# Up projection that begins with two products of each of four column pairs, weight sums of those pairs on VectorE, and the norm's sums held in memory

## The chip, the cores and the metric

The kernel runs on one core of one Trainium2 chip. The metric is the device time of one execution in microseconds, the median of several runs. Inside the core five engines work side by side, each through its own list of instructions in order: TensorE (PE in the rows; its weight loads are PEld), VectorE (DVE), ScalarE (ACT), GpSimd (POOL) and SyncE (SP), which only issues DMA transfers here. They wait for each other through semaphores.

## The reference

One step of a one-layer hybrid encoder for 1024 prompt rows and 32 sample rows, which the kernel handles as 1056 columns of the transposed activations:

```python
h = rmsnorm(x, g_mix); proj = h @ w_in            # attention, short convolution, gates
merged = sigmoid(ga) * y_attn + sigmoid(gc) * y_conv
x = x + merged @ w_o
f = square(relu(rmsnorm(x, g_ffn) @ w_up)) @ w_down   # 1024 -> 4096 -> 1024
x = x + f
x = x + sigmoid(rmsnorm(x, g_ple) @ w_ple_gate) * (p @ w_ple)
y = rmsnorm(x, g_final)
```

All is in float32. The kernel multiplies with three products of split operands (high times high, high times low, low times high).

## The kernel before

Activations stand as 128 features by 1056 columns. A large product is tiled by Strassen's scheme in Winograd's form. For the up projection (`w_up`, 1024 by 4096) 256 output features form a set, 16 sets in all. In a set the weights are four quarters A11, A12, A21, A22 (rows of even and odd feature blocks, and the two halves of 128 output features), and the activations are four quarters B11, B21 (left half of the columns, 528) and B12, B22 (right half). Instead of eight quarter products the set takes seven: A11·B11, S1·T1, S2·T2, A12·B21, S3·T3, S4·B22 and A22·T4. S1 to S4 are sums of weight quarters, made once a set (`prepare`, L203 the sums on POOL, L107/L108 the high and low parts of A11 and A12, L164/L166 those of the sums). T1 to T4 are sums of activation quarters, made once for all sets (`sums` L155, `all_t`, `part_t` L159/L160). A quarter product runs over two quarters of 264 columns; each is 12 matmuls (`products`, L216 to L218) into one PSUM tile, evacuated by ACT (L241, L245, L249) or DVE (L252, L257, L262).

T1 to T4 need all eight rows of the output projection before it (`output_projection`, whose tiles are `ps_wo`, and whose result is stored, squared into `ssq1` and made into B operands by `operands`, L1329/L1330). So the first set does not use the seven products: `up_plain` runs it as eight plain quarter products (tile `ps_up`) while `all_t` makes T1 to T4, and while POOL and ACT prepare set 1. Sets 1 to 15 follow in order, each by `seven`. The results are squared, and further sums of them (`mid_sums`, L1477 to L1485) go to device memory, from where the down projection (`ps_dn`) fetches them.

The order of the work is written by hand: an instruction stands on its engine where the program issues it. `run` takes one step of the main generator (one quarter product with its evacuation), and after each step one step of every generator in the list `side`: preparing the next set's weights, fetching the weights of the set after that, `all_t`, and `mean_squares` (L1450 to L1455), which turns `ssq1` into the norm's factor `rs2` for the down projection. Weight buffers (`raw`, four of 512 KB) and the high and low parts (`whi`, `wlo`, two each) rotate, so a fetch waits until the low part of the older weights is made.

Between the input projection and the attention two tiles of gates are written to device memory (`gd`, L1129), then come the loads of keys, values and queries (`keys_values`, `queries`, L777 to L779).

## Time and profile before

| what | value |
|---|---|
| median of 3 runs | 1541.56 us (1541.32 to 1542.14) |
| profiled execution, its own time | 1541.38 us |
| its span | 1539.7 us |
| PE busy, PEld busy | 1518.7 us, 1506.5 us |
| DVE, ACT, POOL busy | 1067.1, 750.5, 317.6 us |
| up projection, from first ps_up to first ps_dn | 766.36 to 1098.70 us |

The span is the profiler's, from the first to the last instruction; the execution's own time holds 1.7 us more around it. PE is busy nearly throughout, so the table by engine says little: what counts is how far apart matmuls start, and where PE waits.

### The profile page before, as it was taken

How to read it: one execution, taken by the hardware profiler on the slowest of the kernel's cores; microseconds unless marked ns; L12 is line 12 of the kernel's file. 1: busy time of each engine (PE TensorE's matmuls, PEld its weight loads, DVE VectorE, ACT ScalarE, POOL GpSimd, SP SyncE). 2: the span in 40 equal slices, each digit the busy share in tenths (PEclk: the TensorE clock that was granted, in tenths of full speed). 3: DMA queues.
4: the chain of work that ended last, by engine and by line, in shares of the span. 5: the costliest groups of instructions: out<-in, count | busy, mean ns of one | idle time of the engine just before them, and what ended most of it. 6: DMA issues, size and time to landing. Idle time of an engine off the chain costs nothing.

```text
span 1539.7 us, 29459 instructions
## 1 busy us (share of the span) xinstructions
PE 1518.7 (99%) x11816; PEld 1506.5 (98%) x11816; DVE 1067.1 (69%) x1441; ACT 750.5 (49%) x1371; POOL 317.6 (21%) x340
## 2 busy tenths in 40 slices
PE   8999999999999999999999999999999999999997
PEld 7999999999999999999999999999999999999997
DVE  7568656657578887775577555545577986789756
ACT  6544444434456664432355555555543334434644
POOL 2223322231112221002312222221020220000253
PEclk9999999999999999999999999999999999999999
DMA  6513445413748633445354444344886897683433
GB/s 226 202 48 118 187 153 193 166 44 130 236 125 257 207 123 124 147 167 182 128 191 140 146 147 152 131 143 155 303 281 205 279 332 241 198 275 120 141 127 117
DMA packets 110568, 268.94 MB, mean 175 GB/s; under 512 B 12992, under 2 KB 30144, under 8 KB 110432
## 3 DMA queue, kind: packets, MB, share of 16 engines
q1 hardware_dynamic: 110144, 266.75, 51.3%
q8 instruction: 92, 1.51, 0.4%
q14 instruction: 44, 0.36, 0.1%
q10 hardware_dynamic: 288, 0.32, 0.1%
HBM read 186.31 MB, written 80.72 MB: 173 GB/s over the span
## 4 chain that ended last, share of the span: by engine, by line
PE 63%; DVE 0%; ACT 0%; issue 0%; DVEq 0%
PE ps_dn L1696 7%; PE ps_dn L1698 7%; PE ps_dn L1697 7%; PE ps_A11u L217 4%; PE ps_A11u L216 4%; PE ps_A11u L218 4%; PE ps_pg L116 2%; PE ps_wo L1387 2%; PE ps_wo L1386 2%; PE ps_wo L1385 2%; PE ps_pg L118 2%; PE ps_pg L117 2%; PE ps_S1u L217 2%; PE ps_S1u L218 2%; PE ps_S1u L216 2%; PE ps_oa L116 1%
## 5 line engine op out<-in xcount | busy, mean ns | idle before, releaser
L1698 PE MATMUL ps_dn<-fh,wlo_dn 128*128 128x264 f32 x896 | 255.0, 285 | 0.0
L1696 PE MATMUL ps_dn<-fh,whi_dn 128*128 128x264 f32 x896 | 254.8, 284 | 0.0
L1697 PE MATMUL ps_dn<-fl,whi_dn 128*128 128x264 f32 x896 | 254.5, 284 | 0.0
L1696 PEld LDWEIGHTS ps_dn<-fh,whi_dn 128*128 128x128 f32 x896 | 168.8, 188 | 0.0
L1698 PEld LDWEIGHTS ps_dn<-fh,wlo_dn 128*128 128x128 f32 x896 | 168.6, 188 | 0.0
L1697 PEld LDWEIGHTS ps_dn<-fl,whi_dn 128*128 128x128 f32 x896 | 168.6, 188 | 0.0
L203 POOL TENSOR_TENSOR s_i<-raw_i,raw_i 128x512 f32<-128x512 f32 x32 | 43.6, 1363 | 239.9 <-DVE slS_i L166 209.8
L809 DVE TENSOR_TENSOR_SCAN r<-r 128x128 f32<-128x128 f32 (+3 forms) x64 | 86.4, 1351 | 4.1 <-POOL r L802 4.1
L1583 ACT CAST whi_dn<-raw_dn 128x1024 fp32r<-128x1024 f32 x40 | 42.0, 1051 | 83.5 <-PE ps_dn L1697 83.5
L203 POOL TENSOR_TENSOR s_u<-raw_u,raw_u 128x512 f32<-128x512 f32 x30 | 44.1, 1470 | 182.7 <-DVE slS_u L166 171.0
L1589 DVE TENSOR_TENSOR wlo_dn<-raw_dn,whi_dn 128x1024 fp32r<-128x1024 f32 x40 | 61.3, 1532 | 28.4 <-ACT whi_dn L1583 28.4
L216 PE MATMUL ps_A11i<-T,shS_i 128*128 128x264 f32 x256 | 73.1, 285 | 0.0
L218 PE MATMUL ps_A11i<-T,slS_i 128*128 128x264 f32 x256 | 72.9, 285 | 0.0
L217 PE MATMUL ps_A11i<-T,shS_i 128*128 128x264 f32 x256 | 72.7, 284 | 0.0
L849 DVE TENSOR_TENSOR at<-pa,at 128x512 fp32r<-128x512 f32 (+2 forms) x96 | 52.0, 551 | 26.7 <-ACT at L848 22.2
L1609 DVE TENSOR_TENSOR fl<-mr,fh 128x1056 fp32r<-128x1056 f32 x56 | 70.0, 1249 | 0.3 <-ACT q L1649 0.3
L166 DVE TENSOR_TENSOR slS_i<-s_i,shS_i 128x512 fp32r<-128x512 f32 x48 | 35.1, 737 | 49.7 <-ACT shS_i L164 49.5
L802 POOL TENSOR_SCALAR_AFFINE_SELECT r<-r 128x128 f32<-128x128 f32 x64 | 30.4, 475 | 187.8 <-ACT r L795 176.4
L1780 POOL TENSOR_TENSOR xx<-xx,pgs 128x384 f32<-128x384 f32 (+1 forms) x23 | 24.2, 1057 | 216.8 <-DVE pgs L1779 210.1
L216 PE MATMUL ps_A11u<-T,shS_u 128*128 128x264 f32 x240 | 68.4, 285 | 0.0
L217 PE MATMUL ps_A11u<-T,shS_u 128*128 128x264 f32 x240 | 68.4, 285 | 0.0
L218 PE MATMUL ps_A11u<-T,slS_u 128*128 128x264 f32 x240 | 68.1, 284 | 0.0
(451 smaller groups left out, 5582.9 us busy)
## 6 DMA issues: line engine op xcount, KB each, us to landing
raw_dn<-in_w_down_dram SPq DMA_DIRECT2D x56, 512.0 KB, 4.5
raw_i<-in_w_in_dram SPq DMA_DIRECT2D x36, 512.0 KB, 4.6
mr<-mdT SPq DMA_DIRECT2D x32, 528.0 KB, 5.5
raw_u<-in_w_up_dram SPq DMA_DIRECT2D x32, 512.0 KB, 3.5
mdB<-m SPq DMA_DIRECT2D x48, 264.0 KB, 2.5
mr<-mdB SPq DMA_DIRECT2D x24, 528.0 KB, 6.2
raw_pg<-in_w_ple_gate_dram SPq DMA_DIRECT2D x17, 512.0 KB, 3.6
mdT<-ta SPq DMA_DIRECT2D x32, 264.0 KB, 2.1
```

The source lines that it names most:

```text
L116: nc.tensor.matmul(ps, wh, xh[k][:, cols], start=(k == order[0]), stop=False)
L203: f()
L216: nc.tensor.matmul(p_, wh[:, k, :], o[:, 0, c], start=new and n == 0, stop=False, **on)
L217: nc.tensor.matmul(p_, wh[:, k, :], o[:, 1, c], start=False, stop=False, **on)
L218: nc.tensor.matmul(p_, wl[:, k, :], o[:, 0, c], start=False, stop=z, **on)
L809: nc.vector.tensor_tensor_scan(rev, rev, rev, 1.0, ALU.mult, ALU.bypass)
L849: nc.vector.tensor_tensor(al, pt[:, :nb, :], ah.bitcast(F32), op=ALU.subtract)
L1589: dve(lo, raw, hi.bitcast(F32), op=sub)
L1609: dve(l, mraw.pop(v), opd[v].bitcast(F32), op=sub)
L1696: nc.tensor.matmul(ps, hi[:, j, :], oh, start=j == 0, stop=False)
L1697: nc.tensor.matmul(ps, hi[:, j, :], ol, start=False, stop=False)
L1698: nc.tensor.matmul(ps, lo[:, j, :], oh, start=False, stop=j == NP_ - 1)
```

## The change

Four of the sixteen sets (0 to 3) are split in two. `up_early` takes the place of `up_plain`: for each of the four it computes A11·B11 (called P below), keeps a copy in `held_p`, adds A12·B21 into the same PSUM tile (called C), squares the result and writes it out as B11 of that set. The order is P0 P1 C0 C1 P2 C2 P3 C3. Later these four sets run as short sets of five quarter products (S1, S2, S3, S4, A22); the copy P is added or subtracted on DVE. The whole sets stay as they were. The order of sets is 4, 0, 5, 1, 6, 2, 7, 3, then 8 to 15.

For set 4 and for the short sets `prepare` makes the weight sums on DVE in place of POOL, and for the short sets it leaves A11 and A12 out, which `early_split` has split already. Each short set's weights are fetched a second time. `operands` no longer makes B12. `ssq1` is written to device memory and read back 120 steps later for `mean_squares`. The two `gd` writes are issued behind the first two loads of queries.

```diff
-AT1 = (5, 4, 6, 7, 8, 12)
+AT1 = (10, 4, 6, 8, 12, 18)
+AT2 = (0, 4, 6, 8, 10, 13)
+NEARLY = 4
...
         steps = {
-            0: [partial(pool, s3, a11, a21, op=sub)],
-            1: [partial(pool, a21, a21, a22, op=add)],
-            2: [partial(pool, s2, a21, a11, op=sub)],
-            3: [partial(pool, s4, s2, a12, op=sub)],
+            0: [partial(by, s3, a11, a21, op=sub)],
+            1: [partial(by, a21, a21, a22, op=add)],
+            2: [partial(by, s2, a21, a11, op=sub)],
+            3: [partial(by, s4, s2, a12, op=sub)],
         for n, g in zip(at, [first] + parts):
-            steps.setdefault(n, []).append(g)
+            if g is not first or s_ not in held_p:
+                steps.setdefault(n, []).append(g)
...
+    held_p, c11 = {}, {}
+    early_raw, early_w = {}, {}
+
+    def early_fetch(s_, w, n):
+        early_raw[s_] = raw_w(w, n, KD, f"e{s_}")
+
+    def early_split(s_):
+        early_w[s_] = even_odd(load_w(None, 0, KD, f"e{s_}", raw=early_raw.pop(s_)))
+
+    def early_first(s_, t):
+        p_ = early_ps[s_, t] = products(f"e{s_}_{t}", ((early_w[s_][0], "B11"),), quarters[t])
+        nc.scalar.copy(held_p[s_][:, quarters[t]], p_)
+
+    def early_second(s_, t):
+        p_ = early_ps.pop((s_, t))
+        products("", ((early_w[s_][1], "B21"),), quarters[t], p_)
+        return p_
+
+    early_ps = {}
...
+        if s_ in held_p:
+            p1 = [held_p[s_][:, quarters[t]] for t in range(2)]
+            for t, a, b in q:
+                z[t] = product("S1", "T1", t)
+                nc.scalar.copy(s5[t], z[t])
+                yield
+            for t, a, b in q:
+                x[t] = product("S2", "T2", t)
+                nc.scalar.copy(u2[t], x[t])
+                dve(s5[t], s5[t], p1[t], op=sub)
+                yield
...
         for t, a, b in q:
             product("S3", "T3", t, x[t])
+            if s_ in held_p:
+                dve(u2[t], u2[t], p1[t], op=add)
             dve(m2[:, b], x[t], s5[t], op=sub)
             yield
         done("22")
...
         for t, a, b in q:
             product("A22", "T4", t, x[t])
-            last(m2, a, x[t])
+            if s_ in held_p:
+                dve(m2[:, a], x[t], p1[t], op=add)
+                last(m2, a)
+            else:
+                last(m2, a, x[t])
             yield
...
             if s_ + 1 < len(SETS):
                 follow(nm, n, m, 6 * (s_ == 2))
             else:
-                for i in range(2):
-                    nc.sync.dma_start(gd[n + i], m[i])
+                last_m = n, m
...
     with tc.manual_schedule(engines=MM):
         queries(0, 0, 0)
         queries(0, 0, 1)
+        for i, m in enumerate(last_m[1]):
+            nc.sync.dma_start(gd[last_m[0] + i], m)
...
-        by_half = list(zip(halves, ("B21", "B22") if n % 2 else ("B11", "B12")))
-        for c, k in by_half[::-1] if n == KD - 1 else by_half:
+        for c, k in zip(halves, ("B21", "B22") if n % 2 else ("B11",)):
             d, src = operand(k, n // 2), x1[n][:, c]
...
-                fetch_up(n + 2 - KD)
-                prepare_plain("u0", 0)
+                early_split("u0")
         wo_post(KD - 1, 2)
+        early_split("u1")
         wo_after(KD - 1)
...
     def mean_squares():
 
         nonlocal rs2
+        ss = blk("ssb")
+        nc.sync.dma_start(ss, sqd)
+        for _ in range(8):
+            yield
         rs2 = blk("rs2")
         for c in ts:
             ps = tps.tile([P, 512], F32, tag="tp", name=f"ps_ms{c.start}")[:, :TT]
-            nc.tensor.matmul(ps, ones, ssq1[:, c], start=True, stop=True)
+            nc.tensor.matmul(ps, ones, ss[:, c], start=True, stop=True)
...
-    def up_plain():
+    def up_early():
+
+        order = [("P", 0), ("P", 1), ("C", 0), ("C", 1), ("P", 2), ("C", 2), ("P", 3), ("C", 3)]
+        splits = {("C", 0): 2, ("C", 1): 3}
+        for k, i in order:
+            s_ = f"u{i}"
+                if i % 2 == 0:
+                    pair, out = (blk(f"{c}{i}", F32, [P, 2, TH]) for c in ("pe", "ce"))
+                held_p[s_], c11[i] = pair[:, i % 2, :], out[:, i % 2, :]
             for t in range(2):
+                if k == "P":
+                    early_first(s_, t)
+                    p_ = early_second(s_, t)
+                    relu2(c11[i], quarters[t], p_)
+                if t == 1 and (k, i) in splits:
+                    early_split(f"u{splits[k, i]}")
                 yield
+            if k == "C":
+                nc.scalar.square(c11[i], c11[i])
+                nc.sync.dma_start(md("B11", i), c11.pop(i))
...
     def up_set(s_):
         m1, m2 = blk(f"m1_{s_}"), blk(f"m2_{s_}")
+        if s_ < NEARLY:
+            nc.sync.dma_start(m1[:, halves[0]], md("B11", s_))
         sums_ = mid_sums(s_, m1, m2)
...
+            if s_ < NEARLY:
+                next(sums_)
+                side.append(after(1, sums_))
+            else:
+                next(sums_, None)
...
         for j in range(KD // 2 - 1):
             fetch_t(j, 0)
-        side += [prepare("u1", AT1), all_t(), after(3, call(fetch_up, 2))]
-        run(up_plain())
+        early_up(2)
+        early_up(3)
+        seq = [4, 0, 5, 1, 6, 2, 7, 3] + list(range(8, NSET))
+        side += [all_t(), after(1, call(fetch_up, seq[0])), after(3, prepare(f"u{seq[0]}", AT1, dve)), after(7, call(fetch_up, seq[1]))]
+        run(up_early())
         x1.clear()
-        side.append(after(14, mean_squares()))
-        for s_ in range(1, NSET):
-            if s_ + 1 < NSET:
-                side.append(prepare(f"u{s_ + 1}"))
-            if s_ + 2 < NSET:
-                side.append(after(5, call(fetch_up, s_ + 2)))
+        nc.sync.dma_start(sqd, ssq1)
+        side.append(after(120, mean_squares()))
+        for i_, s_ in enumerate(seq):
+            if i_ + 1 < NSET:
+                nx = f"u{seq[i_ + 1]}"
+                side.append(after(6, prepare(nx, AT2, dve)) if seq[i_ + 1] < NEARLY else prepare(nx))
+            if i_ + 2 < NSET:
+                side.append(after(5, call(fetch_up, seq[i_ + 2])))
```

On DVE at the start of the up projection, before, the rows from the first part of T1 on (T is an activation sum, rt its raw form read back, slS the low part of a weight sum, u1 the set, wlo the low part of A11 and A12, w_3 the sums of the last two rows) stand as follows.

```order
L160 TENSOR_TENSOR T1_3_9511<-w_3_9497,T1_3_9511 128x528
L160 TENSOR_TENSOR T1_0_9542<-rt00_9433,T1_0_9542 128x528
L160 TENSOR_TENSOR T1_1_9572<-rt10_9436,T1_1_9572 128x528
L166 TENSOR_TENSOR slS1_u1_9609<-raw_u1_1_9325,shS1_u1_9607 128x512
L160 TENSOR_TENSOR T1_2_9611<-rt20_9439,T1_2_9611 128x528
L108 TENSOR_TENSOR wlo_u1_9641<-raw_u1_0_9323,whi_u1_9640 128x1024
L160 TENSOR_TENSOR T2_3_9644<-w_3_9497,T2_3_9644 128x528
L166 TENSOR_TENSOR slS2_u1_9677<-s2_u1_9493,shS2_u1_9675 128x512
```

And in the changed kernel, on the same engine from the same point (s2, s3, s4 and raw_u4_1 are the weight sums of set 4, eu2 and eu3 the early weights of sets 2 and 3):

```order
L162 TENSOR_TENSOR T1_3_9471<-w_3_9451,T1_3_9471 128x528
L162 TENSOR_TENSOR T1_0_9492<-rt00_9422,T1_0_9492 128x528
L162 TENSOR_TENSOR T1_1_9509<-rt10_9425,T1_1_9509 128x528
L207 TENSOR_TENSOR s3_u4_9513<-raw_u4_0_9474,raw_u4_1_9476 128x512
L162 TENSOR_TENSOR T1_2_9529<-rt20_9428,T1_2_9529 128x528
L207 TENSOR_TENSOR raw_u4_1_9476<-raw_u4_1_9476 128x4x128
L110 TENSOR_TENSOR wlo_eu2_9547<-raw_eu2_9431,whi_eu2_9546 128x1024
L162 TENSOR_TENSOR T2_3_9550<-w_3_9451,T2_3_9550 128x528
L207 TENSOR_TENSOR s2_u4_9512<-raw_u4_1_9476,raw_u4_0_9474 128x512
L162 TENSOR_TENSOR T2_0_9569<-rt00_9422,T2_0_9569 128x528
L207 TENSOR_TENSOR s4_u4_9514<-s2_u4_9512,raw_u4_0_9474 128x512
L110 TENSOR_TENSOR wlo_eu3_9590<-raw_eu3_9433,whi_eu3_9589 128x1024
```

Two of the four weight sums have come in ahead of the low part of eu2, and two more ahead of that of eu3.

On DVE before, from one whole set into the next (ta, m1 and tb are the four sums of results of set 1, slS3_u2 the weight part that set 2's S3 product waits for):

```order
L166 TENSOR_TENSOR slS2_u2_9955<-s2_u2_9755,shS2_u2_9953 128x512
L262 TENSOR_TENSOR m1_1_9723<-u2_u11_9728,ps_S1u1_1_9795 128x264
L166 TENSOR_TENSOR slS3_u2_9987<-s3_u2_9756,shS3_u2_9985 128x512
L1477 TENSOR_TENSOR ta1_9989<-m1_1_9723 128x528
L1479 TENSOR_TENSOR m1_1_9723<-m2_1_9724,m1_1_9723 128x528
L1481 TENSOR_TENSOR ta1_9989<-m1_1_9723 128x528
L1484 TENSOR_TENSOR tb1_9990<-m2_1_9724,ta1_9989 128x528
```

In the changed kernel, from whole set 5 into short set 1:

```order
L168 TENSOR_TENSOR slS2_u1_10428<-s2_u1_10324,shS2_u1_10426 128x512
L1528 TENSOR_TENSOR ta5_10430<-m1_5_10202 128x528
L1530 TENSOR_TENSOR m1_5_10202<-m2_5_10203,m1_5_10202 128x528
L1532 TENSOR_TENSOR ta5_10430<-m1_5_10202 128x528
L1535 TENSOR_TENSOR tb5_10431<-m2_5_10203,ta5_10430 128x528
L168 TENSOR_TENSOR slS3_u1_10478<-s3_u1_10325,shS3_u1_10476 128x512
L270 TENSOR_TENSOR s5_u10_10460<-s5_u10_10460,pe0_9435 128x264
L168 TENSOR_TENSOR slS4_u1_10516<-s4_u1_10326,shS4_u1_10514 128x512
```

All four sums of results now stand ahead of slS3, and the adding of the held copy (pe0) comes between S3's part and S4's.

On SP in the start of the up projection, before (rt01 to rt21 are the raw T3 and T4 read back, raw_u3_0 weights, mdB results):

```order
L98 DMA raw_u3_0_9859<-in_w_up_dram 128x1024
L1352 DMA rt01_9682<-td2_162 128x528
L1352 DMA rt01_9682<-td3_163 128x528
L1352 DMA rt11_9718<-td2_162 128x528
L1352 DMA rt11_9718<-td3_163 128x528
L1506 DMA mdB210_146<-m2_0_9443 128x528
L1352 DMA rt21_9752<-td2_162 128x528
L1352 DMA rt21_9752<-td3_163 128x528
```

In the changed kernel:

```order
L1395 DMA rt01_9572<-td2_163 128x528
L1395 DMA rt01_9572<-td3_164 128x528
L1395 DMA rt11_9596<-td2_163 128x528
L1395 DMA rt11_9596<-td3_164 128x528
L100 DMA raw_u0_0_9603<-in_w_up_dram 128x1024
L100 DMA raw_u0_1_9605<-in_w_up_dram 128x1024
L1559 DMA mdB110_144<-ce0_9436 128x528
L1395 DMA rt21_9628<-td2_163 128x528
L1395 DMA rt21_9628<-td3_164 128x528
```

The last of the raw T3 and T4 now stands behind two weight fetches where there was one.

## Rows read from the trace of the kernel before

**Rows 1.** The page: busy time of TensorE, and the granted clock in 40 slices

```profile
PE 1518.7 (99%) x11816; PEld 1506.5 (98%) x11816; DVE 1067.1 (69%) x1441; ACT 750.5 (49%) x1371; POOL 317.6 (21%) x340
...
PEclk9999999999999999999999999999999999999999
```

**Rows 2.** Stretches: length, busy us (x) of PE, PEld, DVE, ACT, POOL; clock, DMA share, GB/s

```profile
766.00:790.00 24.00, 24.00 (x199) 24.00 (x198) 13.68 (x18) 13.46 (x25) 1.24 (x1) 1.00 0.46 156
...
853.00:874.00 21.00, 21.00 (x175) 21.00 (x174) 10.94 (x17) 11.25 (x23) 6.05 (x5) 1.00 0.42 142
```

**Rows 3.** Instructions of PE in order of time: start us, us, engine, line, operation

```profile
401.37 0.28 PE L661 MATMUL ps_g<-B,wlo_g 128*128 128x264 f32 x1
402.17 0.30 PE L791 MATMUL z<-ks,q 128*128 128x128 f32 x1 [0.52 <-DMA q<-qd]
...
766.36 0.28 PE L216 MATMUL ps_up<-B,whi_u 128*128 128x264 f32 x1
...
789.74 0.28 PE L216 MATMUL ps_A11u<-B,whi_u 128*128 128x264 f32 x1
...
808.61 0.28 PE L218 MATMUL ps_A11u<-T,slA_u 128*128 128x264 f32 x1
808.84 0.39 PE L216 MATMUL ps_A11u<-T,shA_u 128*128 128x264 f32 x1
```

**Rows 4.** One tile's instructions, ps_up: count, duration ns min/median/max, first and last start

```profile
L216 PE MATMUL ps_up<-B,whi_u x64: 279/284/293, 766.4 to 789.4; 128*128 128x264 f32 x64
```

**Rows 5.** Instructions of DVE in order of time, start of the up projection

```profile
769.99 1.25 DVE L1400 TENSOR_TENSOR ssq<-ssq,sq 128x1056 f32<-128x1056 f32 x1
...
772.73 0.77 DVE L155 SCALAR_TENSOR_TENSOR w<-xr,vecT 128x528 f32<-128x528 f32 x1 [1.49 <-ACT xr L1340]
...
775.71 0.70 DVE L160 TENSOR_TENSOR T<-w,T 128x528 fp32r<-128x528 f32 x1
776.32 0.70 DVE L160 TENSOR_TENSOR T<-rt,T 128x528 fp32r<-128x528 f32 x1
```

**Rows 6.** DMA issues of SP in order of time, the two places

```profile
392.83 2.28 SPq L1129 DMA_DIRECT2D gd<-m_i  x2
...
395.68 0.82 SPq L777 DMA_DIRECT2D q<-qd  x1
...
767.52 3.23 SPq L1352 DMA_DIRECT2D rt<-td  x6
770.86 0.36 SPq L98 DMA_DIRECT2D raw_u<-in_w_up_dram  x1
```

**Rows 7.** Tile raw_u, the transfer issued at 770.86: issue to landing

```profile
DMA to landing us min/median/max: 5.7/5.7/5.7
```

**Rows 8.** Tile rt, the two transfers issued at 792.4 and 792.8: issue to landing

```profile
DMA to landing us min/median/max: 4.0/4.1/4.2
```

**Rows 9.** Groups by line and form, 766 to 850 us: count | busy us, mean ns of one

```profile
...
L1455 DVE RECIPROCAL rs<-rs 128x132 f32<-128x132 f32 x8 | 7.6, 962 | 0.0
L159 ACT CAST T<-rt 128x528 fp32r<-128x528 f32 x12 | 7.6, 632 | 2.2 <-DMA mdT<-m 2.2
L108 DVE TENSOR_TENSOR wlo_u<-raw_u,whi_u 128x1024 fp32r<-128x1024 f32 x5 | 6.1, 1211 | 2.5 <-ACT whi_u L107 2.5
L107 ACT CAST whi_u<-raw_u 128x1024 fp32r<-128x1024 f32 x5 | 5.2, 1049 | 4.7 <-PE ps_wo L1386 4.7
L203 POOL TENSOR_TENSOR raw_u<-raw_u 128x512 f32<-128x512 f32 x3 | 3.9, 1299 | 0.2
L166 DVE TENSOR_TENSOR slS_u<-raw_u,shS_u 128x512 fp32r<-128x512 f32 x4 | 2.7, 686 | 2.7 <-ACT shS_u L164 2.7
```

**Rows 10.** DVE and POOL in order of time, sums of one set beside weight sums

```profile
814.64 0.70 DVE L1477 TENSOR_TENSOR ta<-m 128x528 f32<-128x528 f32 x1
815.37 1.67 DVE L1479 TENSOR_TENSOR m<-m,m 128x528 f32<-128x528 f32 x1
```

**Rows 11.** POOL in order of time, the same stretch

```profile
814.86 1.62 POOL L203 TENSOR_TENSOR s_u<-raw_u,raw_u 128x512 f32<-128x512 f32 x1 [0.69 <-DVE slS_u L166]
```

More of the change, by code (lines that the diff above doesn't have):

```diff
@@ L237, in done @@
             after.get(k, int)()
[L239 to L254 removed]
+        if s_ in held_p:
[10 more added lines that the diff above has]
+        else:
+            p1 = [wpool[0].tile([P, TQ], F32, tag="p1", name=f"p1_{s_}{t}") for t in range(2)]
+            for t, a, b in q:
+                x[t] = product("A11", "B11", t)
+                nc.scalar.copy(p1[t], x[t])
+                yield
+            for t, a, b in q:
+                z[t] = product("S1", "T1", t)
+                nc.scalar.copy(s5[t], z[t])
+                yield
+            for t, a, b in q:
+                product("S2", "T2", t, x[t])
+                nc.scalar.copy(u2[t], x[t])
+                yield
+            for t, a, b in q:
+                dve(m1[:, a], product("A12", "B21", t), p1[t], op=add)
+                yield
+            done("11")
         for t, a, b in q:
             product("S3", "T3", t, x[t])
+            if s_ in held_p:
+                dve(u2[t], u2[t], p1[t], op=add)
             dve(m2[:, b], x[t], s5[t], op=sub)
@@ L435, in md @@
         return md_[k, s_ // NP_][s_ % NP_]
+    sqd = dpool.tile([P, T], F32, name="sqd")
     xd = dpool.tile([KD, P, T], F32, name="xd")
```

53 lines of the change are left out of this document (14 added, 39 removed).

## The prediction

> **What bounds the kernel now.** I read the page first: PE is busy 99% of the span at the full clock, the next engine, DVE, 69% [rows 1]. A share of 99% could hide slow stretches, so I looked next at the stretches of the up projection: there PE and PEld are busy without a gap, at the start beside 13.7 us of DVE and 13.5 us of ACT in 24 us, and in a later set with DVE and ACT at little over half [rows 2]. Then I took PE's instructions in order of time. The plain first set has 192 matmuls (three groups of 64 [rows 4]) from 766.36 to 789.74, which is 0.1218 us from one start to the next [rows 3]. In the whole stretch PE loses almost nothing: one start is 0.23 us after the one before it, at 808.84, so 0.11 lost. Outside it one place belongs to the change: at 402.17 the first score matmul comes 0.80 us after its predecessor and waits for a load of queries, 0.68 more than one pace [rows 3]. So the kernel is bound by the number of matmuls, and the change can win only by matmuls it drops and by these two waits. Anything it adds on DVE, ACT, POOL or SP is free until PE reaches an operand that is not ready.
>
> **Matmuls.** A short set saves nothing by itself: two products early and five later are again seven. Early work is 4 sets x 2 products x 2 quarters x 12 = 192 matmuls, as many as the plain set had; later work is 4 x 120 + 12 x 168 = 2496. Before it was 192 + 15 x 168 = 2712, now 2688. The 24 that go are worth 24 x 0.1218 = **2.92 us**. They are on the path whole, since PE is. The wait at 808.84 came from part T4 beside POOL's sums; with the new order I count its **0.11** as gone.
>
> **The queries.** Two writes of gates take SP 2.28 us from 392.83 on, and the query loads start behind them at 395.68 [rows 6]. Now the first two loads of queries go ahead of the writes and start about 2.3 us earlier, more than the 0.68 that PE waits. Next in line is the third query load, which now stands behind the writes, but it serves the third pair of score blocks. I take **0.68**, from 0 (another load is last) to 0.68.
>
> **The first wait, P2.** The early weights rotate through two buffers, so the low part of eu2 can be made only after C0, and P2 needs it. PE reaches P2 after 96 matmuls and wants the low part at the third, 766.36 + 98 x 0.1218 = 778.3. The work on DVE up to there is the old one as far as the addition into ssq1, which starts at 769.99 and ends at 771.2. Behind it come the four sums of the last two rows, 2.98 us (772.73 to 775.71), and three low parts of T1 at 0.61 us pace (775.71 to 776.32) [rows 5]: 776.0. The idle times in that stretch before came from ACT, which had to wait for results of the plain set; the early set gives it none as early. Now stands the first weight sum of set 4, and it needs the second weight tile. Its fetch is issued behind the same six loads of T as a weight fetch before, at 770.86 [rows 6], and that one took 5.7 us [rows 7]: 776.6. No row shows such a sum on DVE. The nearest is the low part of a weight sum, as wide, two inputs in SBUF, 0.69 us with a pace of about 0.61 [rows 5, 9]; the bound from above is POOL's price, 1.30 [rows 9]. I take 0.61. Two sums and one part of T1 end at 778.4, the low part of eu2 takes 1.21 [rows 9]: 779.6. PE waits **1.3 us**; 0.8 if the weights land in time, 2.7 if a sum costs 1.3.
>
> **The second wait, set 4.** From 779.6 DVE does two parts of T2 and two sums, 2.44, and the low part of eu3, 1.21: 783.3. Only then is its weight buffer free, and SP, which works in order, issues a weight fetch, a write of results and the last raw T3, at 0.54 us an issue (3.23 for six [rows 6]): issued at 784.4, and with the 4.0 us of the lone pair before [rows 8] landed at 788.4. On ACT follow its cast 0.63, a copy of half the width 0.3, a cast 0.63 and the high part of set 4's A11 and A12, 1.05 [rows 9], on DVE the low part, 1.21: 792.2. PE, 1.3 late, wants it at the third matmul of set 4: 766.36 + 1.3 + 194 x 0.1218 = 791.3. I take **0.9 us**, from 0 (a landing one microsecond earlier) to 2.3 (sums at 1.3 on DVE).
>
> **The short sets.** S3's low part was due after A11, S1, S2 and A12, that is 8 x 12 matmuls into a set; in a short set it is due after S1 and S2, at 50 x 0.1218 = 6.1 us. Ahead of it on DVE now stand S2's low part and all four sums of the whole set before. While POOL runs a weight sum, DVE stands: the sum that began at 814.64 took 0.70, the next, beside a POOL sum from 814.86 on, 1.67 [rows 10, 11]. POOL makes the next whole set's sums exactly here, released by S1's and S2's low parts, and its third sum can start only when S3's low part is done, so two locks fall in. S2's low part starts about 0.4 us into the set (an estimate: the last parts of S4's result need an addition, two passes of ACT at 0.63 and a half one, and the cast 0.63 behind them, some 3.3 us from a product that ended 2.9 us before). The line is 0.4 + 0.61 + 0.73 + 1.67 + 1.67 + 0.61 + 0.69 = 6.4. PE waits 0.3 us in each of four sets, **1.2 us**; none if ACT is 0.3 us earlier, and 4 x 1.3 = 5.2 if one lock more falls in.
>
> **At nothing.** Each short set has six further additions of 264 columns and two fewer on DVE, 4 x about 0.35 us (a little over half the 0.61 of twice the width), beside two subtractions and casts that it always had; DVE is busy 10.9 us of 21 in a whole set [rows 2]. The norm's sums take eight reciprocals of 0.96 [rows 9] and three matmuls out of sets 2 and 3 into one 120 steps later; the down projection is the first reader. Four weight tiles, four half results and the two transfers of ssq1 add some 4.3 MB to queues that are busy 0.42 of the time [rows 2]. Those rows make some 340 GB/s at a full share, so it is 12.5 us of transfer, which would show if it fell in one place; it is spread over 330 us. B12's parts, no longer made, were off the path.
>
> **The sum.** -2.92 - 0.11 - 0.68 + 1.3 + 0.9 + 1.2 = -0.3. The profiled execution took 1541.38 us (span 1539.7 and 1.7 around it), 0.18 below the median of 1541.56; put on the median the forecast is **1541.3 us**, no change that can be measured: of this kernel a measurement tells 0.2%, 3.1 us. With the smaller bounds of single terms it lies between 1539.3 and 1543.2.
>
> **Rivals.** First, everything is hidden: DVE works ahead, because ACT is idle half of the start, and PE never waits. Then all 3.7 us are won, 1537.8. For it speaks that the early products give ACT little to square; against it, that the line to P2 is one engine's work without idle time in it. Chance 0.15.
>
> Second, the weight sums cost VectorE what they cost POOL, because their inputs have a step between blocks. Place: two sums ahead of eu2, two ahead of eu3, four ahead of each short set's S1. Price: 0.69 a sum, so 1.4 more at P2, 1.4 more at set 4, and 2.8 us in each whole set before a short one, of which I estimate 0.7 to show at S1's low part, four times: 1541.3 + 5.6 = 1546.9, slower. It decides from about 1.1 us a sum. The low parts read the same stepped tiles in 0.69 [rows 9], which speaks against it. Chance 0.13.
>
> Third, the lock: if S2's low part comes a microsecond later, or POOL's sums a little earlier, each short set meets one more lock, 1.3 us, four times: 1546.5. For it speaks how dense DVE's line is there, against it that POOL's third sum is tied to S3's low part. Chance 0.06. The Trainium skill's page "SBUF — State Buffer", section "Who interferes with whom", says that a VectorE instruction with two SBUF inputs and a GpSimd one that reads SBUF exclude each other for the whole instruction. The 1.67 us against 0.70 agrees. By that rule moving sums from POOL to DVE takes a lock away from the short set's own preparation, but the whole sets' sums, which stay on POOL, now fall into the stretch with the nearest due time.
>
> **Chances.** The forecast has 0.66. Faster by over 0.2% needs nearly the whole first rival: 0.13. Slower takes most of the second and third: 0.16. The rest, 0.71, is within 0.2%. The range runs from 1538.4 to 1545.2; what is left out is the first rival's best end and the upper two.
>
> **What the profile after would show.** 24 matmuls fewer between the output and the down projection. No wait at the first score. One wait of about 1.3 us at the third matmul of P2, released by DVE's low part of eu2, one of about 0.9 at set 4's first product, and four of about 0.3 at S3 of the short sets, each on the low part. Weight sums on DVE of 0.7 us. I am wrong if PE waits at none of these places, if a DVE sum takes over 1 us, or if a wait stands at a transfer.

## The result, and the profile after

The changed kernel takes 1544.31 us (median of 19 runs, 1543.30 to 1546.88) where the kernel before takes 1541.29 in the same series (19 runs, 1540.48 to 1542.15): ratio 1.0022, 95% interval 1.0014 to 1.0029. The time lies in the range of the prediction, but it is 3.0 us slower where no change was forecast. The profiled execution took 1546.06 us, with a span of 1544.3.

The page's first view, as in [rows 1], is nearly the same. PE has its 24 matmuls less and is busy 2.5 us longer, but 1.5 of these lie ahead of the first score matmul, in work that the change leaves as it was (394.5 us busy against 393.0), so the page does not show where the loss is; a row of 40 slices is too coarse for it.

```profile
PE 1521.2 (99%) x11792; PEld 1507.4 (98%) x11792; DVE 1090.9 (71%) x1483; ACT 749.8 (49%) x1378; POOL 298.3 (19%) x324
...
PEclk9999999999999999999999999999999999999998
```

Stretches, as in [rows 2], show more. Two of the start of the up projection, of the kernel before and of the one after (length, busy us and count of PE, PEld, DVE, ACT, POOL, then granted clock, DMA share, GB/s):

```profile
772.00:779.00 7.00, 7.00 (x60) 7.00 (x59) 4.22 (x6) 3.83 (x9) 0.00 (x0) 1.00 0.52 191
779.00:785.00 6.00, 6.00 (x52) 6.00 (x51) 2.02 (x3) 3.04 (x7) 0.00 (x0) 1.00 0.13 48
```

```profile
772.00:779.00 7.00, 7.00 (x59) 7.00 (x59) 5.43 (x9) 5.64 (x12) 0.00 (x0) 1.00 0.93 322
779.00:785.00 6.00, 3.79 (x21) 3.58 (x20) 6.00 (x9) 4.37 (x9) 0.00 (x0) 0.76 0.87 298
```

Three things to see: the DMA engines are busy 0.93 and 0.87 where they were busy 0.52 and 0.13; DVE is full from 779 on; and PE makes 21 matmuls in 6 us instead of 52, at a granted clock of 0.76. PE in order of time tells the two losses apart (start, length, engine, line, operation, idle time before it):

```profile
779.15 0.28 PE L241 MATMUL ps_eu<-B,whi_eu 128*128 128x264 f32 x1
781.64 0.39 PE L242 MATMUL ps_eu<-B,wlo_eu 128*128 128x264 f32 x1 [2.21 <-DVE wlo_eu L110]
...
782.50 0.42 PE L241 MATMUL ps_eu<-B,whi_eu 128*128 128x264 f32 x1
782.72 0.42 PE L242 MATMUL ps_eu<-B,wlo_eu 128*128 128x264 f32 x1
...
795.14 0.39 PE L242 MATMUL ps_A11u<-B,wlo_u 128*128 128x264 f32 x1
...
857.57 0.39 PE L242 MATMUL ps_S2u<-T,slS_u 128*128 128x264 f32 x1 [0.51 <-DVE slS_u L168]
```

The first wait is where it was forecast, at the third matmul of P2, but 2.21 us long; counted as the forecast counts it, from when the matmul was due (98 paces behind the first of P0, which starts at 767.30), it is 2.4. From 782.50 to 785.58 matmuls start 0.22 us apart instead of 0.12: PE runs at the lower of its two levels, 1.2 GHz, after it had stood still. Set 4's third matmul, 795.14, comes 0.35 us after the second (0.23 more than a pace). The line at 857.57 is S3 of the second short set, the first of three such waits (857.57, 893.47, 929.42); the first short set has none. DVE's lines ahead of P2, which answer to [rows 5], and SP's, which answer to [rows 6], say why, with the landing of the transfer that SP issues at 771.76:

```profile
775.73 1.32 DVE L162 TENSOR_TENSOR T<-rt,T 128x528 fp32r<-128x528 f32 x2
778.54 0.69 DVE L207 TENSOR_TENSOR s_u<-raw_u,raw_u 128x512 f32<-128x512 f32 x1 [1.50 <-DMA raw_u<-in_w_up_dram]
...
780.37 1.22 DVE L110 TENSOR_TENSOR wlo_eu<-raw_eu,whi_eu 128x1024 fp32r<-128x1024 f32 x1
```

```profile
771.76 0.36 SPq L100 DMA_DIRECT2D raw_u<-in_w_up_dram  x1
772.25 0.41 SPq L1997 DMA_DIRECT2D sqd<-ssq  x1
...
781.92 3.61 SPq L100 DMA_DIRECT2D raw_u<-in_w_up_dram  x2
...
786.10 0.87 SPq L1395 DMA_DIRECT2D rt<-td  x2
```

```profile
DMA to landing us min/median/max: 6.7/6.7/6.7
```

The tile that the first weight sum needs took 6.7 us where [rows 7] had 5.7, and DVE stood 1.50 us for it with the low part of eu2 queued behind. The new write of the norm's sums was issued half a microsecond behind the tile. And SP, in order, stands 3.61 us at the two fetches of set 0 (the second waits for eu3's buffer) with the last two loads of raw T behind them. The weight sum itself takes 0.69.

To compare executions, which start up to 2 us apart, I use three sums of PE's lines: the **delay** at set 4's third matmul (its start less that of the first up matmul, less 194 paces of 0.1218, 23.63 us), the **rest** from there to the first matmul of the down projection, and the stage, which is 23.63 + delay + rest. Before, the delay is 0.00 and the rest 308.71 (stage 332.34). After: delay 4.21, rest 308.30, stage 336.14, 3.80 more. By the forecast the delay was 1.3 + 0.9 = 2.2 and the rest 308.71 - 2.92 - 0.11 + 1.2 = 306.88. Both are over, by 2.0 and 1.4.

### The profile page after: what moved, and what is told of

Same layout as the page of the kernel before. It is cut to its first block, busy times and chain, and to the rows that moved or that the text cites. A ratio compares the mean times of both kernels' runs of the same rounds, so it can differ in the third digit from the quotient of the medians.

```text
span 1544.3 us, 29457 instructions
## 1 busy us (share of the span) xinstructions
PE 1521.2 (99%) x11792; PEld 1507.4 (98%) x11792; DVE 1090.9 (71%) x1483; ACT 749.8 (49%) x1378; POOL 298.3 (19%) x324
## 5 line engine op out<-in xcount | busy, mean ns | idle before, releaser
L207 POOL TENSOR_TENSOR s_u<-raw_u,raw_u 128x512 f32<-128x512 f32 x22 | 33.0, 1498 | 220.6 <-DVE slS_u L168 215.0
L1519 ACT ACTIVATE m<-m 128x528 f32<-128x528 f32 (+1 forms) x52 | 31.8, 611 | 85.5 <-DVE m L287 27.7
L1433 PE MATMUL ps_wo<-mh,wlo_wo 128*128 128x352 f32 x192 | 62.1, 324 | 0.0
L1432 PE MATMUL ps_wo<-ml,whi_wo 128*128 128x352 f32 x192 | 62.1, 323 | 0.0
```

The source lines that it names most:

```text
L207: f()
L1432: nc.tensor.matmul(ps, hi[:, k, :], ml[k][:, c], start=False, stop=False, skip_group_check=True)
L1433: nc.tensor.matmul(ps, lo[:, k, :], mh[k][:, c], start=False, stop=k == KD - 1, skip_group_check=True)
```

## The experiments

The theory at first was: most is lost by the wait at P2 and by the clock that falls behind it, the rest by three waits at S3. Rivals: the line on DVE (or another line) is full and the loss only moves; the weight sums on DVE are too dear; the loss lies in the start of the program. All versions were timed in five rounds beside the kernel before. The table gives what they took, with the wait at P2 (PE's idle time), the landing of set 4's second tile (for e7 that of the transfer of [rows 7]), and delay and rest from their profiled executions. Two ratios here are told apart from about 0.0013 on, 2 us.

| version | median us | ratio to before, interval | landing | wait P2 | delay | rest |
|---|---|---|---|---|---|---|
| e8 unchanged | 1544.84 | 1.0019 (1.0011 to 1.0028) | 7.1 | 2.60 | 4.60 | 308.31 |
| e1 split first | 1543.79 | 1.0011 (1.0002 to 1.0020) | 6.4 | none | 2.39 | 308.17 |
| e2 fill the wait | 1544.80 | 1.0016 (1.0007 to 1.0025) | 6.8 | filled | 3.67 | 308.30 |
| e3 S3 early | 1542.29 | 1.0000 (0.9991 to 1.0009) | 6.2 | 1.65 | 2.97 | 305.29 |
| e4 write later | 1545.46 | 1.0019 (1.0010 to 1.0028) | 6.5 | 2.02 | 4.40 | 308.22 |
| e5 T before weights | 1545.24 | 1.0020 (1.0011 to 1.0030) | 6.7 | 2.19 | 2.72 | 308.34 |
| e6 all three | 1538.01 | 0.9975 (0.9966 to 0.9984) | 6.7 | none | 0.38 | 305.18 |
| e7 before, gates late | 1541.61 | 0.9996 (0.9988 to 1.0005) | 5.3 | none | -0.01 | 308.72 |
| e9 e2 and e5 | 1543.23 | 1.0007 (0.9998 to 1.0015) | 6.4 | filled | 2.40 | 308.31 |
| e10 sums on POOL | 1546.14 | 1.0025 (1.0015 to 1.0035) | 6.6 | moved | 5.66 | 307.94 |
| e11 more writes | 1545.08 | 1.0018 (1.0009 to 1.0026) | 7.1 | 2.61 | 5.38 | 308.30 |
| e12 e6 without e3 | 1540.94 | 0.9991 (0.9982 to 1.0001) | 7.1 | none | 0.47 | 308.19 |
| e13 write from ACT | 1544.23 | 1.0016 (1.0007 to 1.0025) | 5.7 | 1.21 | 3.64 | 308.69 |
| e14 e6 and e13 | 1538.18 | 0.9979 (0.9970 to 0.9988) | 5.6 | none | 0.38 | 305.92 |

**e1, the low part of eu2 ahead of set 4's sums.**

```diff
-AT1 = (10, 4, 6, 8, 12, 18)
+AT1 = (8, 4, 6, 8, 10, 16)
-after(3, prepare(f"u{seq[0]}", AT1, dve))
+after(5, prepare(f"u{seq[0]}", AT1, dve))
```

> Edit: the weight sums of set 4 and its parts start two steps later, so that VectorE makes the low part of eu2 ahead of the first of them. Theory (the first wait and the fall of the clock behind it are most of the loss): the wait of 2.4 us at the third matmul of P2 goes or falls under 0.4, the clock stays at 1.00 in the stretch behind it (0.76 and 0.94 before this edit), which gives 2.4 + 1.6 = 4.0 back; up to 1.0 of it may come back at the parts of eu3 or at set 4's first product, whose line on VectorE starts later. 1540.3 to 1541.3 us, against 1544.3. Rival (the line on VectorE only moves, and the whole of it shows at eu3 or set 4): about 1544. Rival (the loss lies in the start of the program or is spread): 1544 with both places clean.

The wait at P2 is gone and the matmuls behind it keep their pace of 0.12 us, yet the median falls by some 1.2 us only, which the intervals do not tell from none (1.0011 against 1.0019): 2.39 of the delay stays. Two of PE's lines and one of ACT's in this version:

```profile
788.87 0.39 PE L240 MATMUL ps_eu<-B,whi_eu 128*128 128x264 f32 x1 [0.89 <-ACT pe L221]
...
791.62 0.39 PE L242 MATMUL ps_A11u<-B,wlo_u 128*128 128x264 f32 x1 [0.74 <-DVE wlo_u L110]
```

```profile
787.91 0.63 ACT L161 CAST T<-rt 128x528 fp32r<-128x528 f32 x1 [2.00 <-DMA rt<-td]
```

ACT stands 2.00 us for one of the last two loads of raw T. Behind its cast are queued the copy of P3's second result, ahead of which C3 can't add into that PSUM tile (PE waits 0.89), and the high part of set 4's A11, on which the low part rests (0.74). So a second line ends in set 4, and PE feels it as soon as the first is shorter.

**e2, other matmuls in the wait.**

```diff
+                if name == "eu2_0" and n == 0:
+                    fill = tps.tile([P, 512], F32, tag="tp", name="ps_fill")
+                    for _ in range(17):
+                        nc.tensor.matmul(fill[:, :TQ], wh[:, k, :], o[:, 0, c], start=True, stop=True)
                 nc.tensor.matmul(p_, wl[:, k, :], o[:, 0, c], start=False, stop=z, **on)
```

> Edit: 17 matmuls of the same shape, into a PSUM tile that nobody reads, stand between the second and the third matmul of P2 (about 2.1 us of work in the wait of 2.2 us); the output is not touched. The wait stays on the clock on the wall, only PE is not idle in it. Theory (the clock falls because PE stood still): the granted clock of the stretch from the wait to 6 us behind it is 0.98 or more where it was 0.76, no matmul starts 0.22 us after the one before it, and 1.6 us come back: 1542.7. Rival (the clock falls for another reason, such as the load of the other engines or the transfers at that place): the clock still falls, and the time is 1544.3.

The clock stays up, in the profile and, by the mean granted clock of all executions, in the timed ones (0.9977; unchanged 0.9971; before 0.9976). Its stretch from 779 to 785, and set 4's third matmul:

```profile
779.00:785.00 6.00, 5.72 (x47) 5.51 (x46) 6.00 (x10) 4.51 (x9) 0.00 (x0) 1.00 0.85 283
...
793.73 0.39 PE L246 MATMUL ps_A11u<-B,wlo_u 128*128 128x264 f32 x1 [0.75 <-DVE wlo_u L110]
```

By the medians 0.5 us comes back, 1.0016 against 1.0019, with intervals that leave anything from a loss of 1.4 us to a gain of 2.3, so the forecast 1.6 is neither seen nor ruled out. In the profile the delay is 3.67 against 4.21 and 4.60: set 4's matmul now comes 0.91 us behind its pace where it came 0.23 behind, since its operands are late anyway. The theory was right that the clock falls where PE stands still; what the fall costs here stays open. The executions of the unchanged kernel do not settle it either: where the mean granted clock was 0.996 they took 1545.6 (median of five) in the series of the result and 1545.4 (three) in that of e8, where it was 0.998 they took 1543.7 (seven) and 1543.9 (four); but an execution in which the clock falls may also be one with a longer wait, so these 1.5 to 1.9 us are not the clock's alone.

**e3, S3's low part ahead of the sums of the set before.**

```diff
-AT2 = (0, 4, 6, 8, 10, 13)
+AT2 = (0, 3, 5, 6, 10, 13)
```

> Edit: AT2 = (0, 3, 5, 6, 10, 13), so S1's, S2's and S3's parts of a short set are made one to two steps earlier and S3's low part stands on VectorE ahead of the sums of the set before. Theory (three short sets lose 0.65 + 0.1 us each because S3's low part stands behind these sums and the two that POOL holds up): the three waits at S3 go, 2.2 us, 1542.1. Rival (the line is as long in any order, the wait moves to S1's or S2's part or to set 4's low parts): 1544.3, with a wait of the same size at another part.

The three waits at S3 are gone, and with them nearly all small ones behind: the rest falls by 3.0 us, to 305.29. DVE and POOL at the second short set, first unchanged, then in this version (`slS_u` are the low parts, lines 1528 to 1535 the four sums of the set before):

```profile
851.38 0.69 DVE L168 TENSOR_TENSOR slS_u<-s_u,shS_u 128x512 fp32r<-128x512 f32 x1 [2.18 <-ACT shS_u L166]
851.99 0.70 DVE L1528 TENSOR_TENSOR ta<-m 128x528 f32<-128x528 f32 x1
852.72 1.69 DVE L1530 TENSOR_TENSOR m<-m,m 128x528 f32<-128x528 f32 x1
854.44 1.67 DVE L1532 TENSOR_TENSOR ta<-m 128x528 f32<-128x528 f32 x1
856.21 0.71 DVE L1535 TENSOR_TENSOR tb<-m,ta 128x528 f32<-128x528 f32 x1
856.83 0.69 DVE L168 TENSOR_TENSOR slS_u<-s_u,shS_u 128x512 fp32r<-128x512 f32 x1
```

```profile
852.15 1.69 POOL L207 TENSOR_TENSOR s_u<-raw_u,raw_u 128x512 f32<-128x512 f32 x1 [27.05 <-DVE slS_u L168]
853.92 1.63 POOL L207 TENSOR_TENSOR raw_u<-raw_u 128x512 f32<-128x512 f32 x1
```

```profile
848.22 1.72 DVE L168 TENSOR_TENSOR slS_u<-s_u,shS_u 128x512 fp32r<-128x512 f32 x1 [1.57 <-ACT shS_u L166]
849.87 0.69 DVE L1528 TENSOR_TENSOR ta<-m 128x528 f32<-128x528 f32 x1
850.59 1.68 DVE L1530 TENSOR_TENSOR m<-m,m 128x528 f32<-128x528 f32 x1
```

The first of these lines is S3's low part, which begins beside POOL's second sum (848.10, 1.29 us long). The locks are still there (1.72 and 1.68 beside POOL's sums), but S3's part now meets one of them ahead of the sums of the set before and not behind all four. The Trainium skill, "SBUF — State Buffer", section "Who interferes with whom", says that a VectorE instruction with two SBUF inputs contends with a GpSimd one that reads SBUF, and that the shared ports are an exclusive lock. The 1.67 to 1.72 us against 0.69 agree. Delay and wait at P2 were smaller in this execution as well, without the edit touching them (landing 6.2).

**e4, the write later.**

```diff
-        nc.sync.dma_start(sqd, ssq1)
+        side.append(after(2, call(nc.sync.dma_start, sqd, ssq1)))
```

> Edit: the write of the norm's sums to memory, which is issued 0.5 us behind the second weight tile of set 4, is put off until the second step of set 4. Theory (the tile came 1.0 us later than forecast, 6.7 instead of 5.7 us, because that write shares the DMA engines with it): the tile lands in about 5.8 us, VectorE's idle time ahead of the first weight sum falls from 1.5 to 0.5 us, the wait at P2 from 2.4 to about 1.4; whether the clock still falls behind a wait of 1.4 decides between 1543.3 and 1541.7. Rival (the tile is late because of the six loads ahead of it and the last rows' loads, not of the write): it lands in 6.5 us or more, the wait is 2.2 or more, 1544.3.

This told nothing on the write: SP's queue is not ordered by hand, and SP issued it where it had stood, 0.5 us behind the tile (770.94, the tile 770.44). It is one more execution of the unchanged order. With a wait of 2.02 its clock stayed at full speed, and its delay was 4.40 all the same.

**e5, the last loads of raw T ahead of set 0's weights.**

```diff
-after(7, call(fetch_up, seq[1]))
+after(8, call(fetch_up, seq[1]))
```

> Edit: the fetch of the weights of set 0 stands one step later, behind the last two loads of raw T instead of ahead of them; nothing else. Theory (a second line than VectorE's holds set 4: SP stands 3.6 us at that fetch until VectorE has let its buffer go, the last two loads of T are issued behind it, ScalarE waits 2.0 to 2.1 us for them in two of the four runs of the first series, and the copy of P3's result and the high part of set 4's A11 stand behind that on ScalarE): the loads are issued some 3 us earlier, ScalarE does not wait there, the waits at P3's copy (0.94 in the run with the later write) and at set 4's first product (0.75 in all four runs) go to 0.2 or less. The wait at P2 stays at 1.6 to 2.2. From 1.0 to 1.6 us below the unchanged kernel of this series. Rival (set 4's first product only waits because the low parts of eu2 and eu3 are late on VectorE): the 0.75 stays, and the time is that of the unchanged kernel within 0.4.

In the profile the theory holds: ACT has no wait for these loads, set 4's first product loses 0.18, and the delay falls to 2.72 with a wait of 2.19 at P2. The median of all executions did not fall (1.0020). Their mean granted clock is 0.9964, lower than unchanged. The profiled one, which had kept its clock, has 0.997; of the other nine seven have 0.996, one 0.997, and the one with 0.998 is the fastest, 1543.10.

**e9, fill and loads together.** It takes the fall of the clock away from e5.

> Edit: the 17 filling matmuls between the second and third matmul of P2 together with the fetch of set 0 behind the last loads of raw T; the output is not touched. With the late fetch alone the mean granted clock of the timed executions was 0.9964, against 0.9971 unchanged, and the time 1545.24, not faster than unchanged, although its profiled execution, which kept the clock, spent 1.85 us less from the first up matmul to the first down matmul. Theory (the low clock behind P2 has its price, some 1.6 us, but the unchanged kernel does not feel it, since set 4's operands come no earlier; with the late fetch they do, so there it is felt): with the filling the clock is 0.9976 or more, as in before, and the time is 1.3 to 1.8 us below that of the late fetch alone, ratio to before about 1.001. Rival (the clock is not what kept the late fetch from winning): ratio 1.002 as without the filling.

With the clock kept in all executions (0.9977) the ratio is 1.0007: what the filling takes away costs e5 about 2.0 us (1.0020 less 1.0007; the two intervals combined leave 0 to 4), where the 15 or so matmuls at 0.10 us more make 1.5. From the unchanged kernel the same filling takes 0.5, not told from none and not told from 2.0 (e2). That e5 gains more by it, because its operands of set 4 come earlier, is what the theory says and the medians agree with; the intervals do not show it.

**e8, the changed kernel again.**

> The changed kernel without an edit, once more, beside the others. If the low clock behind the wait at P2 is part of what the change costs, this profile shows it again: a granted clock under 0.9 in the 6 us from the wait on, and a wait of over 2 us ahead. If it was one execution's (the run that fills the wait kept its clock, but so did one that waited 2.02 us), the clock is 0.98 or more here, and set 4's first product waits 0.75 instead of 0.23, since PE comes to it earlier. The time stays 0.2% above before.

The low clock came again. Its stretch, and that of e5, from 779 to 785:

```profile
779.00:785.00 6.00, 4.69 (x26) 4.69 (x27) 6.00 (x10) 2.86 (x8) 0.00 (x0) 0.72 0.86 273
```

```profile
779.00:785.00 6.00, 3.81 (x31) 3.60 (x31) 6.00 (x9) 4.64 (x11) 0.00 (x0) 1.00 0.79 252
```

In the profiled executions it fell behind waits of 2.21, 2.60 and 2.61 us at P2, and in e10 behind one of 2.40 at set 4; it stayed behind waits of 0.74 to 2.19. Whether the length of the wait alone decides, these rows don't say. The Trainium skill, "TensorE: Matmul & The Clock Gate", section "HAM oscillation — how this bites in real kernels", says that a wait for data can throw TensorE back to half its clock, paid on top of the wait. These stretches agree on the fall, and the paces of 0.22 us behind it on the price; how much of that price set 4's own wait would have cost anyway is what e2 and e9 leave open.

**e11 and e13, what makes the tile late.** First 1.08 MB more of writes behind the write:

```diff
         nc.sync.dma_start(sqd, ssq1)
+        for i in range(2):
+            nc.sync.dma_start(sqd2[i], ssq1)
```

> Edit: one write of 1.08 MB more (the norm's sums twice, into memory that nobody reads) right behind the write of these sums, 1 us behind the second weight tile of set 4. Theory (the landings are late because the transfers of 20 us share the DMA engines, busy 0.93 and 0.87 of the time from 772 to 785 where they were busy 0.52 and 0.13 before the change): the tile lands in 7.5 to 9 us instead of 6.2 to 7.1, VectorE's idle time grows to 2.3 to 3.8 us and the wait at P2 is that plus 0.7, 3.0 to 4.5; the time rises by 0.8 to 2. Rival (loads land in the order of issue, a write behind the tile does not touch it): it lands in 6.2 to 7.1 us and the wait stays at 1.65 to 2.6.

The tile landed in 7.1 us, at the upper end of what other executions had (6.2 to 7.1 in twelve, this one among them). The wait was 2.61, the time as unchanged: no sign, in one profiled execution, that more behind it makes it later still. Then the write was issued by ACT, some 25 us later:

```diff
-        nc.sync.dma_start(sqd, ssq1)
+        side.append(after(2, call(nc.scalar.dma_start, sqd, ssq1)))
```

> Edit: the write of the norm's sums is issued by ScalarE between set 4's first S1 copies, some 25 us later than by SP. Theory (the write, 0.5 us behind the tile, takes a share of the DMA engines from it): the tile lands in 5.2 to 5.8 us as in the kernel before, VectorE's idle time ahead of the first weight sum is 0.1 to 0.6, the wait at P2 that plus 0.7, 0.8 to 1.3 us; set 4's line through SP still holds its first product, so the time falls by 0.3 to 1 only, ratio to before 1.0013 to 1.0018. Rival (the tile is late by what is ahead of it, or by chance from run to run): it lands in 6.2 to 7.1 us, the wait stays at 1.65 to 2.6, ratio 1.002.

```profile
776.39 0.69 DVE L207 TENSOR_TENSOR s_u<-raw_u,raw_u 128x512 f32<-128x512 f32 x1 [0.49 <-DMA raw_u<-in_w_up_dram]
```

```profile
779.00:785.00 6.00, 5.50 (x45) 5.50 (x46) 6.00 (x10) 5.35 (x11) 0.00 (x0) 1.00 0.95 288
```

The tile lands in 5.7 us, in e14 in 5.6, as in the kernel before (5.7, and 5.3 in e7): without a write right behind it 5.3 to 5.7 in four executions, with it 6.2 to 7.1 in twelve. The theory holds for the tile; the time, 1.0016, is not told from unchanged. Wherever the wait at P2 is not filled or taken away, it is DVE's idle time plus 0.71 to 0.73 (1.50 and 2.21, 0.94 and 1.65, 1.88 and 2.60, here 0.49 and 1.21). The delay stays at 3.64, because set 4's line now ends last: PE waits 1.0 more at C3 for ACT's copy and 0.74 at set 4. ACT's cast of raw T shows what held that line, and the landing of its two loads, issued at 783.95 and 784.38:

```profile
789.73 0.63 ACT L161 CAST T<-rt 128x528 fp32r<-128x528 f32 x1 [2.10 <-DMA rt<-td]
```

```profile
DMA to landing us min/median/max: 5.7/5.8/5.9
```

The Trainium skill, "DMA: Bandwidth & Descriptors", section "Two DMAs through the same engine are not ordered", says that within one queue of one DMA engine descriptors start in order but are pipelined. The tile's 1.0 us for the write right behind it agrees with that; the 7.1 us with two more writes behind is what e11 puts beside it.

**e10, the sums on POOL again.**

```diff
-after(6, prepare(nx, AT2, dve))
+after(6, prepare(nx, AT2))
-prepare(f"u{seq[0]}", AT1, dve)
+prepare(f"u{seq[0]}", AT1)
```

> Edit: one part of the change undone: the weight sums of the four sets ahead of short sets and of set 4 are made by POOL again (the other sets' always are); order and steps unchanged. Theory (a DVE sum of 0.69 is cheap, and it is the order and the landings that cost): at the start POOL needs 4 x 1.3 us and locks VectorE meanwhile, so set 4's S1 part, which now waits for the second sum, and the high parts behind it on ScalarE come 1 to 3 us later, the wait at P2 is about 2 us as now; in the short sets VectorE's line loses four sums of 0.69 but gains locks, the waits at S3 get smaller or go. 1543 to 1547, with a wait of over 1 us at set 4. Rival (the sums on VectorE are what the change pays for): 1541 or less.

The theory holds in the profile: PE waits 1.3, 1.2 and 2.4 us at C2, C3 and set 4 (for ACT's copies of P2 and P3, and for set 4's low part) and no longer at P2, the clock falls behind the last, and the delay is 5.66. The time, 1.0025, is not told from unchanged. But the three waits at S3 shrank to 0.10 or less. So in the short sets the sums on DVE do take part in those waits, which e3's order removes with the sums left on DVE.

**e7, the gates alone, in the kernel before.**

```diff
-                for i in range(2):
-                    nc.sync.dma_start(gd[n + i], m[i])
+                last_m = n, m
...
         queries(0, 0, 1)
+        for i, m in enumerate(last_m[1]):
+            nc.sync.dma_start(gd[last_m[0] + i], m)
```

> Edit: the kernel before with one part of the change alone, the two writes of gates behind the first two loads of queries. Theory: the wait of 0.68 at the first score matmul goes and nothing comes in its place: 0.68 us below before (ratio 0.9996, not told from 1 by a measurement of this kind, so the profile has to show it). Rival (the third load of queries, now behind the writes, or the keys come later instead): a wait of 0.2 to 0.7 at one of the next scores, time as before.

The first score matmul follows its predecessor by one pace (401.98, then 402.10) where it stood idle before [rows 3], and no other wait came up near it. The same holds for the changed kernel (402.11, then 402.23); one later score waits 0.18 us for its keys there (410.36), in e8's profile none. The ratio agrees with 0.68 us but cannot be told from 1.

**e6, e12, e14, the edits together.** e6 is e3's and e5's edits with `AT1 = (7, 4, 6, 8, 10, 16)` behind `after(5, ...)`; e12 is e6 without e3's edit; e14 is e6 with e13's.

> Edit: the three edits together: set 4's weight sums behind eu2's low part, S1's to S3's parts of a short set ahead of the sums of the set before, the fetch of set 0 behind the last loads of raw T. Theory (all that the change loses are these three lines): no wait over 0.3 us in the up projection ahead of the norm's matmuls, granted clock 1.00 from the output projection to the down projection; the time is that of before less the 24 matmuls (2.9), the wait of 0.11 and the queries' 0.68, plus up to 0.8 that remains: 2.9 to 3.7 us below before, ratio about 0.998. Rival (the engines off the path are full, so what is taken away at one place comes back at the next): 1.5 us or less below before, with a wait of 1 us or more at a part of eu3, set 4 or the first short set.

> Edit: the version with all three edits, without that of the short sets. Theory (the short sets' price does not depend on the start): three waits at S3 of 0.65 + 0.1 us and the small ones of 0.1 are back, 2.7 us more than with all three, 1540.7 against 1538.0, ratio to before 0.999; the start shows no wait over 0.3 us. Rival (a late start only moved the short sets' line, and without that the waits at S3 are shorter): under 1.5 us more than with all three.

> Edit: all three edits and the write of the norm's sums from ScalarE. Theory: nothing waits for the tile once eu2's low part stands ahead of the sums (VectorE was idle there for less than 0.1 us with all three edits), so nothing more is won: 1538.0 as with all three, ratio 0.9975; the tile lands in 5.2 to 5.8 us. Rival (the write also holds up the loads of raw T that follow): up to 0.3 us less.

e6 is faster than both kernels, 0.9975, as its theory said: 3.9 us below before, where 2.92 + 0.11 + 0.68 = 3.7 are the three gains of the forecast. PE from 779 to 785:

```profile
779.00:785.00 6.00, 5.95 (x49) 5.74 (x49) 6.00 (x10) 5.43 (x13) 0.00 (x0) 1.00 0.97 309
```

The DMA engines are as full as unchanged, and DVE too; what changed is only which of the things due first stands first. e12 shows that the short sets' price is independent of the start: 308.19 of rest against 305.18, and 0.9991 against 0.9975, 2.5 us. e14 wins nothing over e6; its tile lands in 5.6 us, and nothing waits for it.

## Why the prediction was wrong, point by point

- **24 matmuls, 2.92 us: right.** Without its waits (e6) the rest is 305.18, 3.5 below before: 2.92, two starts late by 0.11 each where the prediction had read one (808.84 and 809.07), and 0.28 at the last of the norm's matmuls (819.49). The prediction's "loses almost nothing" had left these matmuls out: in the kernel before PE loses 1.60 us at them, in e6 1.32.
- **Queries, 0.68: right** in the profiles of e7 and of the changed kernel. The end of the forecast's range was the right value.
- **The first wait, 1.3: the step that failed is its landing.** Place, mechanism and the DVE durations were right (weight sum 0.69, low part 1.22). 5.7 us was taken from a tile that had nothing right behind it [rows 7], but the change itself puts a write of 528 KB right behind this one. That stands in the prediction's paragraph "At nothing": the added 4.3 MB "would show if it fell in one place; it is spread over 330 us". It does fall in one place: DMA is busy 0.93 and 0.87 for 13 us there. One microsecond more of landing is the whole difference between 1.3 and 2.4. With the tile in 5.7 us (e13) the matmul is 1.4 late, as forecast. A wait at a transfer was among the prediction's signs of being wrong, and DVE's 1.50 us is one.
- **The second wait, 0.9: the same step failed again, and this one alone keeps most of the delay.** The last raw T was put at 4.0 us by the two loads of [rows 8]. In e13, where the first wait is as forecast, the low part of eu3 ends 16.9 us behind the first matmul of P0, as forecast, and the first of the two loads is issued at 17.8 (forecast 18.0); but it takes 5.7, and set 4's third matmul is 3.64 late instead of 2.2, 1.4 more. In e1 the two loads took 6.2 and 6.4. In the changed kernel they took 4.6 and 4.8; there the tile's microsecond stands ahead of them, and ACT comes to the cast 0.5 us behind the landing, held by copies and squares of products that PE made late. The delays of the unchanged order are 4.2 to 4.6. e5's edit with e1's, a step earlier still (e12), takes both lines away and leaves 0.47; either alone leaves 2.4 to 2.7. A sum over the waits that one finds in order hides this: each is what is left over by the one before.
- **The clock: a step that was not there.** No term of the forecast allowed for PE's clock behind a wait. In the profile after it costs 15 matmuls some 0.10 us each; e2, which keeps the clock, has 0.5 to 0.9 less of delay. I held it for 1.6 us when I read the profile; the medians put it at 0.5 in the unchanged kernel (e2) and 2.0 in e5 (e9), with intervals too wide to tell the two apart.
- **Short sets, 4 x 0.3: right in kind, too small.** The two locks and the order of DVE were as forecast. In the second short set, which begins at 850.80, S2's low part starts 0.58 us in (forecast 0.4, an estimate), and from there to the end of S3's (851.38 to 857.52) it takes 6.14 (forecast 5.98): 6.7 where 6.1 was due. The waits are 0.64 to 0.69 from one start to the next, less a pace, and 0.1 behind each in three sets; the first has none. With small ones at other parts they make 3.0 (308.30 less 305.29), not 1.2.
- **The sum.** The delay is 2.0 over the forecast, by the two landings, and the rest 1.4: 1.8 by the short sets, less 0.4 that the norm's matmuls and the second late start gave beyond the 0.11. The prediction's narrow range, 1539.3 to 1543.2, leaves out bounds of its own terms: 2.7 and 2.3 for the two waits alone make 1544.1. That the time lies in its wide range, 1538.4 to 1545.2, is luck: that range was made for the rivals, and none of them came true.
- **The rivals.** Everything hidden: false for the change as it is, true for e6. Sums at POOL's price: false, 0.69 us each; with POOL (e10) the delay is 5.66, and the time is no better. A further lock in each short set: not seen, two fell in, as forecast.

What stays open: what makes the two loads of raw T land in 4.6 us in one version and 6.4 in another, since no run changes their neighbours alone; what the fall of the clock costs; why the rest is 0.4 to 0.7 us longer where ACT issues the write (e13, e14); and how long the waits at P2 were in the executions of e5 that were timed and not profiled.

## What to carry to other kernels

Read the DMA share in the stretch that you change, not its mean over the stage, and take a landing only from a transfer with the same neighbours, those issued right behind it included. Where two lines end at nearly the same product, shortening one shows only what the other leaves: follow every line to the same matmul and take the latest, then take both away together. A PE wait may cost more than its length when the clock falls behind it, and less when the next wait was to come anyway: e1 takes the whole wait at P2 away, and 2.39 of 4.2 to 4.6 us of delay stay.

## What was not expected of the hardware

- A write of 528 KB issued 0.5 us behind a load of 512 KB made the load land 0.5 to 1.8 us later (6.2 to 7.1 us in twelve executions; 5.3 to 5.7 in four without it).
- The mean granted clock of a 6 us stretch was 0.76 and 0.72 behind waits of 2.21 and 2.60 us, and 1.00 behind one of 2.19 us; where it fell, matmuls started 0.22 us apart for some 3 us.
- Executions of one program begin the up projection up to 2.0 us apart (765.58 and 767.58 in e8 and e5, which differ only in an edit behind that point), so single profiled times can't be compared to less than that; stages can.
